# A gated convolution with its tokens on the partitions, two opening blocks that take turns, and a warm-up on a constant, in a two-layer decoder kernel

## Chip, cores and metric

One core of a Trainium2 chip runs the whole program. The metric is the device time of one execution in microseconds (us). The kernel before takes 259.68 us, the median of 3 runs (259.32 to 259.75).

## What is computed

Two layers on x (256 tokens, 1024 wide, fp32). Each layer normalizes its input, multiplies it by a wide input matrix, mixes, gates with a SiLU and multiplies by an output matrix; the result is added to x. Layer 0 mixes by a causal convolution of three taps, layer 1 by causal attention over 256 tokens (16 heads of 64, with normalized q and k and a distance bias).

```python
def short_conv_mixer(h, w_in, conv_w, w_out):
    b_gate, c_gate, xv, z = split(h @ w_in, 4)
    u = c_gate * xv
    conv = conv_w[0] * u[t-2] + conv_w[1] * u[t-1] + conv_w[2] * u[t]
    y = b_gate * conv * silu(z)
    return y @ w_out
```

## The kernel before

**Units and products.** All weights are cut into 80 units of 256 rows by 512 columns (`UNITS`, L23); four units make a block, which fills two PSUM banks, one for each half (t = 0, 1) of the tokens. Every fp32 operand is split into a high part that TensorE reads as it is and a low part: ScalarE (ACT) copies the high part (`whi`, L355), VectorE (DVE) subtracts it from the loaded weights (`wlo`, L362). Each unit then takes 12 products of 128x512: high by high, high by low and low by high, for two k tiles and two token halves (L419 to L421; L405 for the first unit). Layer 0 has 32 units of the input matrix in two halves (`hf`) of four blocks each, C, x, gate and B, then 8 of the output matrix; layer 1 likewise with 32 and 8.

**The convolution before.** A block's products leave tokens on the partitions. `scaled` (L475) and `times` (L480) make u = C times x; `conv` (L502) turns u with 8 transposes on TensorE (PE, L451), so that columns stand on the partitions and tokens along the row, and a shift by one or two tokens is an offset in the row: ScalarE multiplies by one tap (L512), VectorE adds the other two (L520). `gated` (L533) turns B times SiLU in another 8 transposes, multiplies (L539) and splits the result into high and low `ys` (L493, L497), the input of the output matrix.

**What sets the order.** The kernel records every operation with its engine, a cost, and what it reads and writes; `Plan.schedule` (L164) simulates the engines and fixes one order for each engine. On the chip each engine takes its instructions in exactly that order, and each waits on semaphores for what it needs. Buffers are rings: 4 of 1 MiB for loaded weights (`raw`, a pair of units each), 5 units each for `whi` and `wlo`. All transfers are issued by SyncE (SP), from one queue: first x, as eight transposed k tiles, with the first four units (L298), then pairs of units (L314), with x again, tokens on the partitions, as `h` between (L325).

**The start.** Eight products of zeros (`WARM`, L273) run before data is there. `zero` is written by VectorE (L270).

Of the kernel before, what the change touches and what calls it, by code (L numbers as in the profile page):

```python
# [8 lines left out]
F32 = mybir.dt.float32  # L9
# [24 lines left out]
NSM = 48  # L34
# [168 lines left out]
def hybrid_kernel(  # L203
    ctx: ExitStack,
    tc: tile.TileContext,
    first: bass.AP,
    xt: bass.AP,
# [45 lines left out]
    sm = one.tile([P, NSM], F32, name="sm")  # L253
# [3 lines left out]
    zero = one.tile([P, 512], mybir.dt.bfloat16, name="zero")  # L257
    one.tile([P, 16], F32, name="fill")
# [3 lines left out]
    kk2 = one.tile([P, 2, 4, 2, S], F32R, name="kk2")  # L262
    kT, klz = kk2[:, :, :, 0], kk2[:, :, :, 1]
    qT = one.tile([P, 2, 4, S], F32R, name="qT")
    vv = one.tile([P, 2, 4, 4, HD], F32R, name="vv")
    g0, g1, taps = sm[:, 0:8], sm[:, 8:16], sm[:, 16:40]
# [16 lines left out]
    firsts = [raw_t() for _ in range(4)]  # L283
    raws = {g: raw_t() for g in range(2, NU // 2)}

    def piece(k, a, b):
        o = 768 * (k % 2) + (NSM if k < 2 else 0)
        return firsts[k // 2]().rearrange("p a b -> p (a b)")[:, o + a : o + b]


    def load_first(k, parts="xw"):
        a, b = (0 if "x" in parts else S), (768 if "w" in parts else S)
        if k == 0 and a == 0:
            a = -NSM
        op(
            "SP",
            max(us(P * 4 * (b - a)), 480),
            lambda: sp.dma_start(piece(k, a, b), first[:, NSM + 768 * k + a : NSM + 768 * k + b]),  # L298
            w=[(firsts[k // 2], (k % 2, p)) for p in parts],
        )  # L300


    def w_in(u, ks):
        if u >= 4:
# [3 lines left out]
        return (firsts[u], (k, "w")), lambda: piece(2 * u + k, S, 768).rearrange("p (k f) -> p k f", f=512)  # L308

    def load_pair(g):  # L310
        op(
            "SP",
            us(P * 8192),
            lambda: sp.dma_start(raws[g](), w[2 * g - 4 : 2 * g - 2].rearrange("u p e -> p u e")),  # L314
            w=[(raws[g], 0), (raws[g], 1)],
        )

    load_first(0, "x")
    load_first(0, "w")
    for k in range(1, KT):  # L320
        load_first(k)
    op("DVE", 80, lambda: dve.tensor_copy(sm, piece(0, -NSM, 0)), r=[(firsts[0], (0, "x"))], w=["sm"])
    load_pair(2)
    for t in range(2):
        op("SP", us(P * 4096), lambda t=t: sp.dma_start(h[:, t], xt[:, t]), w=[("h", t, 0), ("h", t, 1)])  # L325
    for g in range(3, NU // 2):
        load_pair(g)
# [12 lines left out]
    for s in range(2):  # L340
        r2 = slice(HD - s * HD, P - s * HD)
        op("POOL", 950, lambda s=s, r2=r2: pool.memset(klz[r2, s].bitcast(F32), 0.0), w=[("klz0", s)])
# [4 lines left out]
    def split(u, parts=1):  # L347
        for i in range(parts):
# [18 lines left out]
    def split_x(k):  # L367
        key = [(firsts[k // 2], (k % 2, "x"))] + (["sm"] if k else [])
        g = lambda: g0[:, k : k + 1] if k else piece(0, -NSM, 1 - NSM)
        op(  # L370
            "ACT",
            500,
            lambda: act.activation(xs[:, k, 0], piece(k, 0, S), AF.Copy, scale=g()),  # L373
            r=key,
            w=[("xs", k, 0)],
        )
        op(
            "DVE",
            480,
            lambda: dve.scalar_tensor_tensor(  # L380
                xs[:, k, 1], piece(k, 0, S), g(), xs[:, k, 0].bitcast(F32), op0=ALU.mult, op1=ALU.subtract
            ),
            r=key + [("xs", k, 0)],
            w=[("xs", k, 1)],
        )
# [4 lines left out]
    def dense(kp, banks, x, xname):  # L390
        u = unit[0]
        unit[0] += 1
        if u < 4:
            for k in (2 * kp, 2 * kp + 1):
                split_x(k)
        split(u, 2 if u < 4 else 1)

        last = u == NU - 1


        def first_products(kk):
            wh, wl = his[u]()[:, kk], los[u]()[:, kk]
            for n, (i, m) in enumerate(((0, wh), (1, wh), (0, wl))):
                for t in range(2):
                    pe.matmul(  # L405
                        banks[t](), lhsT=x[:, kk, i, t * P : (t + 1) * P], rhs=m, start=(kk == 0 and n == 0), stop=False
                    )
# [15 lines left out]
        steps = [[(0, kk), (1, kk)] for kk in range(2)]  # L423
        if last:
            steps = [[(0, 0)], [(0, 1)], [(1, 0, 0), (1, 1, 0)], [(1, 0, 1), (1, 1, 1)]]
        for tk in steps:
# [3 lines left out]
                lambda tk=tk: first_products(tk[0][1]) if u == 0 else [product(*a) for a in tk],  # L430
# [60 lines left out]
    def split_y(y, j0, nj):  # L491
        js = range(j0, j0 + nj)
        op("ACT", 150 + 250 * nj, lambda: act.copy(ys[:, j0 : j0 + nj, 0], y()[:, 0:nj]), r=[y], w=[("ys", j, 0) for j in js])  # L493
        op(
            "DVE",
            180 + 280 * nj,
            lambda: dve.tensor_sub(ys[:, j0 : j0 + nj, 1], y()[:, 0:nj], ys[:, j0 : j0 + nj, 0].bitcast(F32)),  # L497
            r=[y] + [("ys", j, 0) for j in js],
# [3 lines left out]
    def conv(hf, i, us_):  # L502
        j0 = 4 * hf + 2 * i
        bank = transposed(lambda t: us_[t](), us_, [2 * i * P, (2 * i + 1) * P])
        c = bias_t()
        for jj in range(2):
            j = j0 + jj
            b = lambda jj=jj: bank()[:, jj * S : (jj + 1) * S]
            op(
                "ACT",  # L510
                440,
                lambda b=b, j=j, jj=jj: act.activation(c()[:, jj], b(), AF.Copy, scale=taps[:, 16 + j : 17 + j]),  # L512
                r=[bank, "sm"],
                w=[(c, jj)],
            )
            for d in (1, 2):
                op(
                    "DVE",
                    460,
                    lambda b=b, j=j, jj=jj, d=d: dve.scalar_tensor_tensor(  # L520
                        c()[:, jj, d:S],
                        b()[:, 0 : S - d],
                        taps[:, 8 * (2 - d) + j : 8 * (2 - d) + j + 1],
                        c()[:, jj, d:S],
                        op0=ALU.mult,
                        op1=ALU.add,
                    ),
                    r=[bank, "sm"],
                    w=[(c, jj)],
                )  # L530
        return c

    def gated(hf, i, c, qs):  # L533
        bank = transposed(lambda t: qs[t](), qs, [2 * i * P, (2 * i + 1) * P])
        y = y_t()
        op(
            "DVE",
            700,
            lambda: dve.tensor_mul(y(), c(), bank().rearrange("p (j s) -> p j s", s=S)),  # L539
            r=[(c, 0), (c, 1), bank],  # L540
            w=[y],
        )
        split_y(y, 4 * hf + 2 * i, 2)

    for hf in range(2):
        banks = block(xs, "xs")
# [3 lines left out]
        banks = block(xs, "xs")  # L550
        us_ = [times(banks[t], t, cs[t]) for t in range(2)]
        convs = [conv(hf, i, us_) for i in range(2)]
        banks = block(xs, "xs")
        sl = [scaled(banks[t], t, AF.Silu) for t in range(2)]
        banks = block(xs, "xs")
        qs = [times(banks[t], t, sl[t]) for t in range(2)]
        for i in range(2):
            gated(hf, i, convs[i], qs)
# [54 lines left out]
    def small_ones():  # L613
        dve.tensor_scalar(epsv, v1, EPS, None, op0=ALU.mult)
        dve.tensor_mul(gg, sm[:, 40:41], sm[:, 41:42])
# [11 lines left out]
    def queries_or_keys(name, bank, t):  # L627
# [30 lines left out]
        for s in range(2):  # L658
            r, r2 = slice(s * HD, s * HD + HD), slice(HD - s * HD, P - s * HD)
            if name == "k":  # L660
                hi = kT[r, s, :, ts]
                op("ACT", 680, lambda r=r, hi=hi: act.activation(hi, psv()[r], AF.Copy, scale=gg[r]), r=[tb, "gg"], w=[("k", t, s, 0)])
# [4 lines left out]
                        klz[r, s, :, ts], psv()[r], gg[r], hi.bitcast(F32), op0=ALU.mult, op1=ALU.subtract  # L667
                    ),
                    r=[tb, "gg", ("k", t, s, 0)],
                    w=[("kl", t, s)],  # L670
                )
                op("POOL", 640, lambda r2=r2, s=s, hi=hi: pool.tensor_copy(kT[r2, s, :, ts], hi.bitcast(F32)), r=[("k", t, s, 0)], w=[("k", t, s, 1)])
            else:
                hi = qT[r, s, :, ts]
                op("ACT", 600, lambda r=r, hi=hi: act.copy(hi, psv()[r]), r=[tb], w=[("q", t, s, 0)])
# [3 lines left out]
                    lambda r=r, r2=r2, s=s, hi=hi: dve.tensor_sub(qT[r2, s, :, ts], psv()[r], hi.bitcast(F32)),  # L679
                    r=[tb, ("q", t, s, 0)],  # L680
                    w=[("q", t, s, 1)],
# [34 lines left out]
    def pair(j, s2):  # L716
# [7 lines left out]
        def scores():  # L724
            for s in range(2):
                a, b, o = qT[:, s, jj, 0:P], qT[:, s, jj, P:S], sc[s]()
                o1 = o[:, 0:S].rearrange("p (i k) -> p i k", k=P)
                pe.matmul(o1, lhsT=a, rhs=kk2[:, s, jj, :, 0:P], start=True, stop=True)
                pe.matmul(o[:, S:512], lhsT=b, rhs=kT[:, s, jj], start=True, stop=False)  # L729
# [206 lines left out]
```

## Time and profile before

| what | us |
|---|---|
| runs: median (lowest to highest) | 259.68 (259.32 to 259.75) |
| the profiled execution, its own time | 259.06 |
| its span | 257.3 |
| PE busy | 251.8 |
| DVE busy | 188.7 |
| ACT busy | 163.3 |
| POOL busy | 49.7 |

The span runs from the first instruction of the program to the last; the execution's own time has 1.8 us more around it. Busy times add up each engine's instructions; they overlap, and an idle engine costs nothing if nobody waits for it. In a timeline row the first number is the start, the second the time, and what stands in brackets is how long the engine sat idle before, and what ended that. PE is TensorE's products, PEld its weight loads; SPq is the queue that issues transfers.

### The profile page before, as it was taken

To read this page: it belongs to the slowest core of one execution; us is meant where nothing else is said; L and a number is where in the kernel's file an instruction comes from. 1 tells how busy PE (TensorE), PEld (TensorE's weight loads), DVE (VectorE), ACT (ScalarE), POOL (GpSimd) and SP (SyncE) were. 2 spreads that over 40 slices of the span, in tenths; PEclk is the share of its full clock that TensorE was granted. 3 is DMA by queue.
4 is the path that set the end of the run, shared out by engine and by line. 5 is a ranking of instruction groups with operands and counts; after the bars stand their busy time and mean duration, and the time that the engine had idled before them with its cause. 6 is when DMAs were issued, how large, how long until landed. Compare 5 with 4: busy or idle time off the path is not lost.

```text
span 257.3 us, 3436 instructions
## 1 busy us (share of the span) xinstructions
PE 251.8 (98%) x1198; PEld 206.8 (80%) x1198; DVE 188.7 (73%) x335; ACT 163.3 (63%) x286; POOL 49.7 (19%) x76
## 2 busy tenths in 40 slices
PE   8999999999999999999999999999999999999994
PEld 3688888888888888888888888888888888888873
DVE  2874985575558458667767976984999899977973
ACT  4868655345445535474557668996887777988720
POOL 5001000000000000000636511242164901045230
PEclk9999999999999999999999999999999999999999
DMA  6999985554666444654655454053094504400004
GB/s 216 398 395 416 383 318 164 167 171 161 225 223 201 163 163 163 176 190 173 227 169 211 138 191 163 3 169 157 3 284 152 219 3 164 164 0 3 0 0 163
DMA packets 12657, 45.33 MB, mean 176 GB/s; under 512 B 864, under 2 KB 1248, under 8 KB 12640
## 3 DMA queue, kind: packets, MB, share of 16 engines
q1 hardware_dynamic: 12640, 45.12, 49.6%
q8 instruction: 9, 0.15, 0.2%
q14 instruction: 8, 0.07, 0.1%
HBM read 44.06 MB, written 1.05 MB: 175 GB/s over the span
## 4 chain that ended last, share of the span: by engine, by line
PE 87%; DVE 4%; ACT 3%; DMA 2%; issue 1%; POOLq 0%; SPq 0%; POOL 0%
PE mm L421 26%; PE mm L419 26%; PE mm L420 26%; DMA raw<-in_first_dram 2%; PE at L451 2%; PE at L799 2%; PE at L653 1%; DVE wlo L362 1%; DVE y L838 1%; ACT whi L355 1%; PE at L820 1%; ACT prob L761 1%; DVE pp L806 1%; PE at L730 1%; PE at L729 1%
## 5 line engine op out<-in xcount | busy, mean ns | idle before, releaser
L362 DVE TENSOR_TENSOR wlo<-raw,whi 128x1024 fp32r<-128x1024 f32 (+1 forms) x84 | 98.0, 1175 | 43.0 <-ACT whi L355 42.7
L355 ACT CAST whi<-raw 128x1024 fp32r<-128x1024 f32 (+1 forms) x84 | 84.5, 1012 | 69.7 <-PE mm L421 56.5
L419 PE MATMUL mm<-whi,xs 128*128 128x512 f32 x252 | 100.3, 398 | 0.2 <-ACT xs L373 0.2
L421 PE MATMUL mm<-whi,xs 128*128 128x512 f32 x252 | 98.5, 391 | 0.0
L420 PE MATMUL mm<-wlo,xs 128*128 128x512 f32 x252 | 98.3, 390 | 0.0
L421 PEld LDWEIGHTS mm<-whi,xs 128*128 128x128 f32 x252 | 47.3, 188 | 10.4 <-DVE xs L380 0.2
L419 PEld LDWEIGHTS mm<-whi,xs 128*128 128x128 f32 x252 | 47.4, 188 | 9.4 <-ACT xs L373 0.6
L420 PEld LDWEIGHTS mm<-wlo,xs 128*128 128x128 f32 x252 | 47.4, 188 | 9.0
L419 PE MATMUL mm<-whi,ys 128*128 128x512 f32 (+1 forms) x64 | 25.4, 397 | 0.0
L421 PE MATMUL mm<-whi,ys 128*128 128x512 f32 (+1 forms) x64 | 24.9, 389 | 0.3 <-POOL ys L844 0.3
L420 PE MATMUL mm<-wlo,ys 128*128 128x512 f32 (+1 forms) x64 | 24.7, 386 | 0.0
L459 POOL TENSOR_TENSOR stat<-stat,nhalf 128x2 f32<-128x2 f32 x2 | 1.4, 709 | 118.1 <-DVE stat L458 118.1
L838 DVE TENSOR_TENSOR y<-at,y 64x256 f32<-64x256 f32 x32 | 13.5, 421 | 4.6 <-ACT y L836 3.8
L721 POOL TENSOR_SCALAR bias<-dist 128x256 f32<-128x256 f32 x16 | 9.1, 569 | 30.5 <-DVE sums L751 28.5
L761 ACT ACTIVATE prob<-neg,sums 128x256 f32<-128x256 f32 (+1 forms) x32 | 14.3, 449 | 1.0 <-DVE sums L751 0.9
L421 PEld LDWEIGHTS mm<-whi,ys 128*128 128x128 f32 x64 | 12.0, 188 | 3.2 <-POOL ys L844 0.7
L420 PEld LDWEIGHTS mm<-wlo,ys 128*128 128x128 f32 x64 | 12.1, 188 | 2.1
L419 PEld LDWEIGHTS mm<-whi,ys 128*128 128x128 f32 x64 | 12.0, 188 | 2.0
L635 POOL TENSOR_TENSOR ss<-ss,nhalf 128x8 f32<-128x8 f32 x8 | 13.1, 1641 | 0.7
L844 POOL TENSOR_TENSOR ys<-y,ys 128x256 fp32r<-128x256 f32 x8 | 7.7, 962 | 18.1 <-ACT ys L840 18.1
L775 POOL TENSOR_TENSOR sg<-row,sums 128x128 f32<-128x128 f32 x16 | 7.1, 463 | 16.9 <-ACT row L711 10.6
L802 ACT CAST pp<-at 128x384 fp32r<-128x384 f32 x16 | 7.5, 480 | 2.0 <-PE at L799 1.9
(95 smaller groups left out, 260.8 us busy)
## 6 DMA issues: line engine op xcount, KB each, us to landing
raw<-in_w_dram SPq DMA_DIRECT2D x38, 1024.0 KB, 4.9
raw<-in_first_dram SPq DMA_DIRECT2D x7, 384.0 KB, 6.5
h<-in_x_dram SPq DMA_DIRECT2D x2, 512.0 KB, 8.2
out_dram<-row SPq DMA_DIRECT2D x3, 256.0 KB, 2.5
raw<-in_first_dram SPq DMA_DIRECT2D x1, 256.0 KB, 2.7
out_dram<-row SPq DMA_DIRECT2D x2, 128.0 KB, 2.2
raw<-in_first_dram SPq DMA_DIRECT2D x1, 152.0 KB, 2.6
```

The source lines that it names most:

```text
L355: lambda c=c, src=src: act.copy(his[u]()[:, c], src()),
L362: lambda c=c, src=src: dve.tensor_sub(los[u]()[:, c], src(), his[u]()[:, c].bitcast(F32)),
L419: pe.matmul(o, lhsT=a, rhs=wh, start=(k == first_k), stop=False)
L420: pe.matmul(o, lhsT=a, rhs=wl, start=False, stop=False)
L421: pe.matmul(o, lhsT=b, rhs=wh, start=False, stop=(k == KT - 1))
L635: pool.tensor_tensor(ss()[:, 8:16], ss()[:, 0:8], nhalf, op=ALU.pow)
L721: op("POOL", 450, lambda s=s, slope=slope: pool.tensor_scalar(b()[:, s], dist, slope, 1.0, op0=ALU.mult, op1=ALU.mult), r=["dist", "epsv"] ...
L761: lambda s=s, c=c, i=i, neg=neg: act.activation(p[s]()[:, c], neg()[:, c], AF.Exp, bias=sums()[:, i : i + 1], scale=-1.0, accum_out=sums() ...
L775: lambda t=t: pool.tensor_mul(sg()[:, t].rearrange("p (s d) -> p s d", d=HD), s2[t]()[:, jj * P : (jj + 1) * P].rearrange("p (s d) -> p s ...
L802: op("ACT", 480, lambda s=s, tb=tb: act.copy(pp()[:, s, 0], tb()[:, 0:384]), r=[tb], w=[(pp, (s, 0))])
L838: op("DVE", 430, lambda s=s, r=r, c=c: dve.tensor_add(y()[r, 1], av[s]()[r, c], y()[r, 1]), r=[av[s]], w=[(y, s)])
L844: lambda: pool.tensor_sub(ys[:, j, 1], y()[:, 0], ys[:, j, 0].bitcast(F32)),
```

## The change

**Start.** The first two blocks (units 0 to 3 and 4 to 7) take turns over the first four k tiles; then each runs its last two units alone. The first six units and x are loaded in pieces in the order of the table `FIRST`, where `x3` is a k tile of x and `(4, 1)` the second k tile of unit 4. The high part of k tile 0 is made by VectorE. The warm-up reads a constant of the program in place of `zero`.

**Convolution.** u stays as it comes, tokens on the partitions. A shift by d tokens is now a shift by d partitions, made by transfers inside SBUF: the "main" one moves 128 - d rows of 4 KB (both token halves), the "head" one d rows of 2 KB across the halves. Taps come from HBM, copied to every partition (1.5 MiB), and VectorE multiplies and adds on 128x1024. The gate follows, and one group of 8 transposes for each half remains, whose result goes straight to `ys`. The 8 transposes of u, L512 and L520 are gone.

```diff
+NF = 6
+FIRST = [
+    [[(0, 0)], ["p", "x0"], [(4, 0)]],
+    [["x1", (0, 1)], [(4, 1), "x2"]],
...
+    [["x6", (3, 0)], ["x7", (3, 1)]],
+]
-    dve.memset(zero, 0.0)
+    ones = lambda n: nc.const_aps.tensor(1.0, [P, n], mybir.dt.bfloat16)
-        pe.matmul(idle, lhsT=zero[:, 0:P], rhs=zero, start=True, stop=True)
+        pe.matmul(idle, lhsT=ones(P), rhs=ones(512), start=True, stop=True)
+    op("SP", us(P * 12288), lambda: sp.dma_start(early()[:, 0:3072].bitcast(F32), taps_b), w=[(early, "taps")])
...
+    def conv(hf, banks, cs):
...
+                    u_at(t), banks[t](), r0[:, t : t + 1], cs[t](), op0=ALU.mult, op1=ALU.mult
...
+        for d in (1, 2):
+            op(
+                "SP",
+                1400,
+                lambda d=d: sp.dma_start(u_before(d)[d:P], u_both()[0 : P - d]),
...
+            op(
+                "SP",
+                480,
+                lambda d=d: sp.dma_start(u_before(d)[0:d, 1], u_at(0)[P - d : P]),
...
+                lambda d=d: dve.tensor_mul(u_before(d), u_before(d), tb(2 - d)),
...
+        op("DVE", 1230, lambda: dve.tensor_mul(u_both(), u_both(), tb(2)), r=[(early, "taps")], w=[(early, ("u", t)) for t in range(2)])
...
+            lambda: dve.tensor_add(u_before(1), u_before(1), u_before(2)),
...
+            lambda: dve.tensor_add(u_before(1), u_before(1), u_both()),
...
+    def gated(hf, sl):
...
+                lambda t=t: dve.tensor_mul(sl[t](), sl[t](), u_before(1)[:, t]),
...
+    def output(hf, i, ys_):
+        bank = transposed(lambda t: ys_[t](), ys_, [2 * i * P, (2 * i + 1) * P])
...
+        op("ACT", 620, lambda: act.copy(ys[:, j0 : j0 + 2, 0], ps()), r=[bank], w=[("ys", j, 0) for j in js])
...
+    def first_blocks():
+        both = [[mm_t(), mm_t()] for _ in range(2)]
+        for k in range(4):
+            for i in range(2):
+                dense(k // 2, both[i], xs, "xs", 4 * i + k // 2, k % 2)
+        for i in range(2):
+            for kp in (2, 3):
+                dense(kp, both[i], xs, "xs", 4 * i + kp)
```

**Order on SP, before.** The whole queue of transfers; `raw` is the weight ring, `row` the output.

```order
L298 DMA raw<-in_first_dram 128x512
L298 DMA raw<-in_first_dram 128x304
L298 DMA raw<-in_first_dram 128x768 x7
L314 DMA raw<-in_w_dram 128x2x1024 x2
L325 DMA h<-in_x_dram 128x1024 x2
L314 DMA raw<-in_w_dram 128x2x1024 x36
L883 DMA out_dram<-row 128x512 x3
```

Every transfer here has 128 rows, one for each partition.

**Order on SP, changed,** from the last opening piece on. `kk` holds the taps and u, `qq` the shifted copies of u.

```order
L346 DMA raw<-in_w_dram 128x2x1024
L356 DMA h<-in_x_dram 128x1024 x2
L346 DMA raw<-in_w_dram 128x2x1024 x5
L354 DMA kk<-in_taps_dram 128x3072
L556 DMA qq<-kk 2x512
L549 DMA qq<-kk 126x1024
L556 DMA qq<-kk 1x16x32
L549 DMA qq<-kk 127x1024
L346 DMA raw<-in_w_dram 128x2x1024 x9
L549 DMA qq<-kk 127x1024
L556 DMA qq<-kk 1x16x32
L549 DMA qq<-kk 126x1024
```

The taps and the four shifts of the first half stand behind the pair of units 16 and 17, those of the second half behind the pair of units 34 and 35; 22 pairs follow.

**Order on DVE, before,** from the first u (L485) to the first gate (L539) of the first half.

```order
L485 SCALAR_TENSOR_TENSOR row<-mm,stat,row 128x512 x2
L362 TENSOR_TENSOR wlo<-raw,whi 128x1024 x3
L520 SCALAR_TENSOR_TENSOR bias<-at,sm,bias 128x255 x4
L362 TENSOR_TENSOR wlo<-raw,whi 128x1024
L520 SCALAR_TENSOR_TENSOR bias<-at,sm,bias 128x254 x3
L362 TENSOR_TENSOR wlo<-raw,whi 128x1024
L520 SCALAR_TENSOR_TENSOR bias<-at,sm,bias 128x254
L362 TENSOR_TENSOR wlo<-raw,whi 128x1024 x4
L485 SCALAR_TENSOR_TENSOR row<-mm,stat,row 128x512 x2
L362 TENSOR_TENSOR wlo<-raw,whi 128x1024
L539 TENSOR_TENSOR y<-bias,at 128x512
```

Nothing between u and the gate reads a transfer inside SBUF; L520 reads what PE has turned.

**Order on DVE, changed,** around the convolution of the first half: L539 makes u, L566 to L581 the taps, L591 the gate, L525 is B times that.

```order
L539 SCALAR_TENSOR_TENSOR kk<-mm,stat,row 128x512 x2
L390 TENSOR_TENSOR wlo<-raw,whi 128x1024 x4
L566 TENSOR_TENSOR qq<-qq,kk 128x1024
L390 TENSOR_TENSOR wlo<-raw,whi 128x1024
L566 TENSOR_TENSOR qq<-qq,kk 128x1024
L570 TENSOR_TENSOR kk<-kk 128x1024
L574 TENSOR_TENSOR qq<-qq 128x1024
L581 TENSOR_TENSOR qq<-qq,kk 128x1024
L591 TENSOR_TENSOR row<-row,qq 128x512 x2
L525 SCALAR_TENSOR_TENSOR row<-mm,stat,row 128x512 x2
L390 TENSOR_TENSOR wlo<-raw,whi 128x1024 x4
```

The first L566 reads the shift by two tokens, the second the shift by one. The splits (L390) ahead of L539 end with unit 12, the one between the two L566 is that of unit 17, and the first behind L525 that of unit 18. On PE the 8 transposes that read L525's result stand behind unit 16 in the first half and behind unit 32 in the second.

**Order on DVE, changed,** at the same place of the second half.

```order
L566 TENSOR_TENSOR qq<-qq,kk 128x1024
L390 TENSOR_TENSOR wlo<-raw,whi 128x1024
L566 TENSOR_TENSOR qq<-qq,kk 128x1024
L390 TENSOR_TENSOR wlo<-raw,whi 128x1024
L570 TENSOR_TENSOR kk<-kk 128x1024
L390 TENSOR_TENSOR wlo<-raw,whi 128x1024
L574 TENSOR_TENSOR qq<-qq 128x1024
L581 TENSOR_TENSOR qq<-qq,kk 128x1024
L591 TENSOR_TENSOR row<-row,qq 128x512 x2
L390 TENSOR_TENSOR wlo<-raw,whi 128x1024 x3
L525 SCALAR_TENSOR_TENSOR row<-mm,stat,row 128x512 x2
```

Here the first L566 reads the shift by one token, and the split behind it is that of unit 30; the three ahead of L525 are those of units 33 to 35.

## Rows read from the trace of the kernel before

**Rows 1.** The page: busy times, and the chain that ended last by engine.

```profile
PE 251.8 (98%) x1198; PEld 206.8 (80%) x1198; DVE 188.7 (73%) x335; ACT 163.3 (63%) x286; POOL 49.7 (19%) x76
...
PE 87%; DVE 4%; ACT 3%; DMA 2%; issue 1%; POOLq 0%; SPq 0%; POOL 0%
```

**Rows 2.** Timeline of PE, first 10 us: start, time, instruction, [idle before].

```profile
1.17 3.60 PE L273 MATMUL at<-zero 128*128 128x512 bf16 x8 [1.17 <-DVE nhalf L330]
4.57 1.96 PE L405 MATMUL mm<-whi,xs 128*128 128x512 f32 x4
...
8.78 0.50 PE L419 MATMUL mm<-whi,xs 128*128 128x512 f32 x1 [0.17 <-ACT xs L373]
...
9.83 0.39 PE L419 MATMUL mm<-whi,xs 128*128 128x512 f32 x1
```

**Rows 3.** Timeline of ACT: high parts of the weights (L355), and what they waited for.

```profile
14.88 2.00 ACT L355 CAST whi<-raw 128x1024 fp32r<-128x1024 f32 x2 [1.41 <-DMA raw<-in_w_dram]
17.44 2.00 ACT L355 CAST whi<-raw 128x1024 fp32r<-128x1024 f32 x2 [0.56 <-DMA raw<-in_w_dram]
...
22.50 1.05 ACT L355 CAST whi<-raw 128x1024 fp32r<-128x1024 f32 x1 [0.97 <-DMA raw<-in_w_dram]
...
28.42 1.06 ACT L355 CAST whi<-raw 128x1024 fp32r<-128x1024 f32 x1 [0.87 <-PE mm L421]
...
42.95 1.05 ACT L355 CAST whi<-raw 128x1024 fp32r<-128x1024 f32 x1 [0.51 <-PE mm L421]
45.67 1.05 ACT L355 CAST whi<-raw 128x1024 fp32r<-128x1024 f32 x1 [1.67 <-PE mm L421]
48.39 1.05 ACT L355 CAST whi<-raw 128x1024 fp32r<-128x1024 f32 x1 [1.67 <-PE mm L421]
```

**Rows 4.** Timeline of PE around the first transposes of u (L451).

```profile
30.95 1.04 PE L451 MATMUL at<-ident,row 128*128 128x128 f32 x8
31.74 0.47 PE L419 MATMUL mm<-whi,xs 128*128 128x512 f32 x1
32.05 0.39 PE L420 MATMUL mm<-wlo,xs 128*128 128x512 f32 x1
```

**Rows 5.** The DMA view: all packets, then issues with KB each and us to landing.

```profile
DMA packets 12657, 45.33 MB, mean 176 GB/s; under 512 B 864, under 2 KB 1248, under 8 KB 12640
...
raw<-in_w_dram SPq DMA_DIRECT2D x38, 1024.0 KB, 4.9
raw<-in_first_dram SPq DMA_DIRECT2D x7, 384.0 KB, 6.5
h<-in_x_dram SPq DMA_DIRECT2D x2, 512.0 KB, 8.2
out_dram<-row SPq DMA_DIRECT2D x3, 256.0 KB, 2.5
raw<-in_first_dram SPq DMA_DIRECT2D x1, 256.0 KB, 2.7
out_dram<-row SPq DMA_DIRECT2D x2, 128.0 KB, 2.2
raw<-in_first_dram SPq DMA_DIRECT2D x1, 152.0 KB, 2.6
```

**Rows 6.** Busy times by stretch: PE, PEld, DVE, ACT, POOL, granted clock, DMA share, GB/s.

```profile
20.00:26.00 6.00, 6.00 (x28) 4.95 (x28) 2.60 (x4) 5.03 (x9) 0.72 (x1) 1.00 1.03 420
...
38.00:60.00 22.00, 22.00 (x103) 18.28 (x102) 13.80 (x16) 10.25 (x12) 0.00 (x0) 1.00 0.55 183
```

**Rows 7.** Groups of DVE by form, first 110 us: count, busy, mean ns, idle before.

```profile
L362 DVE TENSOR_TENSOR wlo<-raw,whi 128x1024 fp32r<-128x1024 f32 x37 | 44.9, 1223 | 30.9 <-ACT whi L355 30.8
L485 DVE SCALAR_TENSOR_TENSOR row<-mm,stat,row 128x512 f32<-128x512 f32 x8 | 5.6, 744 | 0.0
...
L539 DVE TENSOR_TENSOR y<-bias,at 128x512 f32<-128x512 f32 x4 | 2.7, 684 | 1.7 <-PE at L451 1.7
```

**Rows 8.** Timeline of DVE: two splits in a row.

```profile
25.68 2.36 DVE L362 TENSOR_TENSOR wlo<-raw,whi 128x1024 fp32r<-128x1024 f32 x2 [0.87 <-ACT whi L355]
```

More of the change, by code (lines that the diff above doesn't have):

```diff
@@ L206, in hybrid_kernel @@
     first: bass.AP,
+    taps_b: bass.AP,
     xt: bass.AP,
@@ L256, in hybrid_kernel @@
     stat = one.tile([P, 24], F32, name="stat")
-    zero = one.tile([P, 512], mybir.dt.bfloat16, name="zero")
-    one.tile([P, 16], F32, name="fill")
+    one.tile([P, 272], F32, name="fill")
     h = one.tile([P, 2, DM], F32, name="h")
@@ L279, in us, with item, load_first @@
         return nbytes / 370
[L283 to L294, printed above, removed]
+    firsts = [raw_t() for _ in FIRST]
+    raws = {g: raw_t() for g in range(NF // 2, NU // 2)}
+    where = {}
+    base = 0
+    transfers = []
+    for f, groups in zip(firsts, FIRST):
+        o = 0
+        for group in groups:
+            o0 = o
+            for item in group:
+                where[item] = f, o, item_size(item)
+                o += item_size(item)
+            transfers.append((f, o0, o, base + o0, group))
+        base += o
+    def item(name):
+        f, o, n = where[name]
+        return f().rearrange("p a b -> p (a b)")[:, o : o + n]
+    def load_first(f, o0, o1, at, group):
         op(
             "SP",
-            max(us(P * 4 * (b - a)), 480),
-            lambda: sp.dma_start(piece(k, a, b), first[:, NSM + 768 * k + a : NSM + 768 * k + b]),
-            w=[(firsts[k // 2], (k % 2, p)) for p in parts],
+            max(us(P * 4 * (o1 - o0)), 480),
+            lambda: sp.dma_start(f().rearrange("p a b -> p (a b)")[:, o0:o1], first[:, at : at + o1 - o0]),
+            w=[(f, i) for i in group],
         )
     def w_in(u, ks):
-        if u >= 4:
+        if u >= NF:
             g = raws[u // 2]
@@ L388, in hybrid_kernel, with dense @@
     unit = [0]
-    def dense(kp, banks, x, xname):
-        u = unit[0]
-        unit[0] += 1
+    def dense(kp, banks, x, xname, u=None, only=None):
+        if u is None:
+            u = unit[0]
+            unit[0] += 1
         if u < 4:
-            for k in (2 * kp, 2 * kp + 1):
+            for k in (2 * kp, 2 * kp + 1) if only is None else (2 * kp + only,):
                 split_x(k)
-        split(u, 2 if u < 4 else 1)
+        split(u, 2 if u < NF else 1, only)
         last = u == NU - 1
[L401 to L407, printed above, removed]
         def product(t, kk, half=None):
@@ L421, in product @@
             pe.matmul(o, lhsT=b, rhs=wh, start=False, stop=(k == KT - 1))
-        steps = [[(0, kk), (1, kk)] for kk in range(2)]
+        if only is not None and 2 * kp + only == 0:
+            wh, wl = lambda: his[u]()[:, 0], lambda: los[u]()[:, 0]
+            for n, (i, m, parts) in enumerate(((0, wh, his), (1, wh, his), (0, wl, los))):
+                op(
+                    "PE",
+                    454,
+                    lambda n=n, i=i, m=m: [
+                        pe.matmul(banks[t](), lhsT=x[:, 0, i, t * P : (t + 1) * P], rhs=m(), start=(n == 0), stop=False)
+                        for t in range(2)
+                    ],
+                    r=[(parts[u], 0), (xname, 0, i)],
+                    w=banks,
+                    rank=1,
+                )
+            return
+        steps = [[(0, kk), (1, kk)] for kk in ((0, 1) if only is None else (only,))]
         if last:
@@ new lines, in gated @@
+    def gated(hf, sl):
+        for t in range(2):
+            op(
+                "DVE",
+                700,
+                lambda t=t: dve.tensor_mul(sl[t](), sl[t](), u_before(1)[:, t]),
+                r=[(shifted, (1, p)) for p in ("zero", "main", "head")],
+                w=[sl[t]],
+            )
+    def output(hf, i, ys_):
+        bank = transposed(lambda t: ys_[t](), ys_, [2 * i * P, (2 * i + 1) * P])
+        j0 = 4 * hf + 2 * i
+        ps = lambda: bank().rearrange("p (j s) -> p j s", s=S)
+        js = (j0, j0 + 1)
+        op("ACT", 620, lambda: act.copy(ys[:, j0 : j0 + 2, 0], ps()), r=[bank], w=[("ys", j, 0) for j in js])
```

221 lines of the change are left out of this document (118 added, 103 removed).

## The prediction

> **What bounds the kernel now.** I read the page first: PE is busy for 251.8 of 257.3 us and carries 87% of the chain that ended last [rows 1]. A change can therefore gain only by taking work off PE or by filling the places where PE waits, and can lose by making PE wait. The next question is where it waits. In the timeline of PE the eight warm-up products start 0.43 us apart (3.40 us from 1.17 to 4.57), and the first 15 products (12 of L405 and three more), from 4.57 to 9.83, take 5.26 us [rows 2]. From then on the pace is that of the units: ScalarE starts a new split every 2.72 us, each time released by PE, which has freed a buffer [rows 3]. So a unit of 12 products takes 2.72 us, one product 0.227 us, and the opening 15 products would take 3.4 us at that pace: 1.9 us are lost at the start. After the start loads and splits are ahead of PE (ScalarE waits for PE, not for data, from 28.42 on [rows 3]), and PE is full in both stretches shown, the second of which is convolution [rows 6]. Last the DMA view and the stretches: from 20 to 26 us the transfers run at full rate, 420 GB/s on all 16 DMA engines (share 1.03), from 38 to 60 us at about half [rows 6].
>
> **The start.** The second block gives PE six more products for each k tile that arrives, in the very gap where it now waits (0.17 us before 8.78, and the slow pace around it [rows 2]). Bounds: nothing, if the lower pace of the first products simply lasts longer; 1.9 us, if all is recovered. I take 1.0: the first product still needs the first piece and its high part, and the first products still come at the slow pace. Dropping `zero` lets the warm-up begin up to 0.4 us earlier; this is inside the same bound. The copies, pieces and the extra DVE operation for k tile 0 lie beside loads that are late anyway.
>
> **PE work of the convolution.** Each of the two halves loses one group of 8 transposes. A group takes 0.79 us from its start to the next product (30.95 to 31.74), and that product then takes 0.31 us instead of 0.23 to the next [rows 4]: 0.87 us, twice, is 1.75 us. PE is full there, so all of it counts. The ScalarE copies and VectorE multiply-adds that go are off the path, and both engines have idle time there [rows 6]; they are costed at nothing.
>
> **The shifts.** This is the added wait. The DVE operation on a shifted copy waits for a transfer issued by SP, and behind it on DVE stand the splits of later units and, at last, the operation that PE's remaining transposes need. What does a shift by one token cost? It moves 127 rows of 4 KB. No row of the trace moves 127 rows, so I bound it. The trace has 54 transfers (38+7+2+3+1+2+1) and 864 packets under 512 B [rows 5]: 864 is 54 times 16, one closing packet from each of the 16 DMA engines for every transfer. All have 128 rows, so each engine gets an equal share of 8. At 420 GB/s an engine moves 26 GB/s [rows 6], a row of 4096 B in 0.156 us. If 127 rows are spread as 128 are, the shift moves in 8 x 0.156 = 1.3 us. If shares must be equal in whole rows, 127, a prime number, has only one engine to go to: 127 x 0.156 = 19.8 us. I take 19.8, because equal shares are what all 54 transfers show; the 126 rows of the other shift then go to 14 engines, 9 each, 1.4 us. The Trainium skill says the same from another side: by "DMA: Bandwidth & Descriptors", section "Why a DMA increments its semaphore by 16 and not by 1", a transfer uses the largest number of engines, up to 16, that divides the outermost dimension, and it names 127 partitions as a case for one engine. The trace agrees for 128 rows and cannot show 127; by that rule the sum below is 287, with the nearest rows taken as they stand it is 257.
>
> **First half.** Bytes ahead of the pair of units 8 and 9 are as before, so it lands near 22.5 again [rows 3]; a pair is 1.05 MB, 2.5 us at 420 GB/s. Units 10 to 17 follow until 32.5, the taps (1.57 MB) until 36.2, then the shift by two (1.4 us), then the 127 rows: 37.6 + 19.8 = 57.4. u is earlier than that: unit 7 ends at 28.4 - 1.0 = 27.4 [rows 3], then come the high part (1.05 [rows 3]) and low part (1.2 [rows 7]) of unit 12, and u itself (2 x 0.74 [rows 7]), 31.2 in all, so the queue and not u sets the shift. VectorE goes on from 57.4 with four operations on 128x1024 (1.18 each, as two splits in a row take 2.36 [rows 8]), two of 0.69 and two of 0.74 us [rows 7], together 7.6: 65.0. PE reaches the transposes after unit 16, at 27.4 + 9 x 2.72 = 51.9. It waits 13.1 us.
>
> **Second half.** After the transposes (0.87) PE does units 17 to 23 (19.0), 84.9; with a slower restart (below, 1.3) 86.2. u takes 1.5, 87.7. The shift by one is first in its group now and the queue is half empty [rows 6]: 128 KB land 2.2 us after issue, of which 0.3 is moving [rows 5], so 1.9 + 19.8 later, 109.4. DVE stands at this shift; the split of unit 30 is behind it. From there to the operand of the transposes are five operations and six splits of 1.18 and four short ones, 15.9 us: 125.3. PE would have come to them, after units 24 to 32, at 86.2 + 24.5 = 110.7. It waits 14.6 us.
>
> **Restart.** After a wait of 13 us PE may come back at the pace of the start, 0.43 us a product. The start bounds this: from 1.17 until at most 6.5 us it ran so [rows 2], half of which is lost: between 0 and 2.6 us at each of two waits; I take 1.3. The Trainium skill, "TensorE: Matmul & The Clock Gate", section "Part 1: The HAM clock gate", says that idleness puts the clock back to half; no row here shows it after the start. Without that the sum would be 2.6 less.
>
> **Sum.** -1.0 - 1.75 + 13.1 + 14.6 + 2.6 = +27.6. The profiled execution took 259.06 us, so 286.6; the median of the runs is 0.6 above it, so I forecast **287 us**. Layer 1 is reordered slightly by the planner; I cost that at nothing, because PE's products there are the same.
>
> **The range of this case.** Low: both restarts free (-2.6), the start wholly recovered (-0.9), and the 127 rows begun alongside the taps and not after them (-5.1): 278. High: rows that take a third longer inside SBUF than from HBM (13 in two shifts) and the full restart (2.6): 302.
>
> **Rivals.**
> 1. *The 127 rows go to all 16 engines, unevenly.* Then a shift lands near 36.2 + 2 x 1.3 = 38.8. DVE wants it after the low part of unit 17, whose buffer is free after unit 12 (27.4 + 5 x 2.72 = 41.0, plus 1.05 and 1.2): 43.3. Nothing waits, the sum is -2.75, and the time 256.9: faster. For it: every row of the trace uses all 16. Against: every row is a multiple of 16.
> 2. *Spread, but late all the same.* VectorE needs 7.6 us from 43.3, 50.9, and PE is there at 51.9: a margin of 1.0 us. If queueing behind weights and taps delays the shift beyond 44.4, each us more is a us on PE; from 47 on the gain is gone. A shift at 48 would give about 260: the same, or slower. Against: it must land 9 us later than its bytes need.
> **How the numbers follow.** One engine: 0.83. Rival 1: 0.11. Rival 2: 0.04. The rest, 0.02, is something slower still. A measurement of this kernel tells about 0.2% from no change, 0.5 us. Faster is rival 1 and a little: 0.11; the same, out of rival 2: 0.02; slower: 0.87. The range 278 to 302 holds nearly all of the first case, 0.79 in all, so it needs no stretch to 257.
>
> **What would show it.** The SP-issued L549 with 127 rows should land some 20 us after it starts moving, and DVE should sit idle before L566 until about 57 and 109. PE should stand before L491 near 52 and 111. The DMA share should fall far below 0.5 in these stretches, and PE's next products should come 0.43 us apart. The L491 groups should be two in place of four, and unit 7 should end near 27.4. If L549 lands within 3 us, the forecast is wrong by its main term, and 257 is the time; if PE waits but far less than 27 us in sum, the place of the shift in the queue was wrong.

## The result: 13.6% slower

The changed kernel takes **294.79 us** (median of 4 runs, 294.58 to 295.09) against 259.50 of the kernel before, measured beside it (4 runs): a ratio of 1.136, 95% interval 1.134 to 1.138. The forecast was 287 (278 to 302), slower with a chance of 0.87. The profiled execution took 294.58, with a span of 292.8.

The page of the changed kernel: busy times, the granted clock in 40 slices, the DMA share, the chain that ended last (by engine, then by line), and three groups (busy, mean ns | idle before, releaser).

```profile
PE 255.7 (87%) x1182; PEld 208.5 (71%) x1182; DVE 194.9 (67%) x330; ACT 160.2 (55%) x279; POOL 55.8 (19%) x81
...
PEclk9999999755899997589999999999999999999999
...
DMA  6999918900746251048564464540704372530003
...
PE 52%; DMA 24%; DVE 13%; issue 4%; ACT 3%; SPq 2%; POOLq 0%; POOL 0%; DVEq 0%; ACTq 0%
DMA qq<-kk 18%; PE mm L445 15%; PE mm L443 15%; PE mm L444 15%; DVE wlo L390 4%; DMA raw<-in_w_dram 3%; DMA raw<-in_first_dram 2%; DVE y L920 2%; PE at L491 2%; PE at L881 1%; ACT whi L383 1%; PE at L735 1%; DVE kk L539 1%; DVE qq L566 1%; DVE qq L581 1%
...
L444 PE MATMUL mm<-wlo,xs 128*128 128x512 f32 x252 | 100.2, 398 | 12.6 <-DVE wlo L390 12.6
...
L566 DVE TENSOR_TENSOR qq<-qq,kk 128x1024 f32<-128x1024 f32 x4 | 4.9, 1222 | 39.5 <-DMA qq<-kk 39.5
...
L491 PE MATMUL at<-ident,row 128*128 128x128 f32 x16 | 3.5, 359 | 18.4 <-DVE row L525 18.3
```

PE carried 87% of the chain [rows 1]; now it carries 52, and the shifts (`qq<-kk`) alone 18. VectorE waits 39.5 us for two of them, and PE 12.6 + 18.3 us for VectorE. The holes in the DMA line and the two dips of PEclk mark the places. PE's busy time grew although 16 transposes went: part of its products ran at the lower clock (0.5 in the rows below, 1.2 GHz; 1.00 is 2.4 GHz).

The chain of waits in order of time, around both shifts (start, us, what):

```profile
34.61 27.74 DMA qq<-kk
62.37 1.23 DVE qq L566
...
94.30 24.94 DMA qq<-kk
```

The second of these is the head of the second half, 2 KB: issued right behind the 127 rows (93.62), its last share landed at 119.24, 0.2 us after theirs (119.05).

Four stretches (PE, PEld, DVE, ACT, POOL busy, granted clock, DMA share, GB/s):

```profile
39.00:45.00 6.00, 6.00 (x29) 4.95 (x27) 3.71 (x4) 3.27 (x4) 0.00 (x0) 1.00 0.07 26
...
53.00:62.00 9.00, 0.09 (x1) 0.00 (x0) 0.00 (x0) 0.00 (x0) 0.00 (x0) 0.62 0.66 232
62.00:69.00 7.00, 0.00 (x0) 0.00 (x0) 6.56 (x7) 3.64 (x4) 1.03 (x2) 0.50 0.07 28
...
109.00:119.00 10.00, 0.19 (x1) 0.00 (x0) 0.00 (x0) 1.04 (x1) 0.00 (x0) 0.71 0.22 79
```

From 39 to 45 us only the shift moves: 26 GB/s and a share of 0.07, one engine of sixteen (1/16 is 0.06). [Rows 6] had 420 GB/s at 1.03.

The timeline of SP there: start, us, the transfers that it issues.

```profile
34.61 1.43 SPq L549 DMA_DIRECT2D qq<-kk  x1
36.14 11.20 SPq L346 DMA_DIRECT2D raw<-in_w_dram  x2
...
93.62 0.63 SPq L549 DMA_DIRECT2D qq<-kk  x1
94.30 9.11 SPq L556 DMA_DIRECT2D qq<-kk  x1
```

The timeline of DVE: the operations on the shifted copies, with the idle time before each in brackets.

```profile
62.37 1.23 DVE L566 TENSOR_TENSOR qq<-qq,kk 128x1024 f32<-128x1024 f32 x1 [17.81 <-DMA qq<-kk]
...
119.36 1.22 DVE L566 TENSOR_TENSOR qq<-qq,kk 128x1024 f32<-128x1024 f32 x1 [21.65 <-DMA qq<-kk]
```

The timeline of ACT in the first half, the first split of weights after the shift was issued and its wait:

```profile
64.90 1.99 ACT L383 CAST whi<-raw 128x1024 fp32r<-128x1024 f32 x2 [21.59 <-DMA raw<-in_w_dram]
```

The timeline of PE around the first wait:

```profile
52.71 0.39 PE L445 MATMUL mm<-whi,xs 128*128 128x512 f32 x1
69.27 2.32 PE L491 MATMUL at<-ident,row 128*128 128x128 f32 x8 [16.17 <-DVE row L525]
71.24 0.78 PE L443 MATMUL mm<-whi,xs 128*128 128x512 f32 x1
71.81 0.63 PE L444 MATMUL mm<-wlo,xs 128*128 128x512 f32 x1
72.24 0.63 PE L445 MATMUL mm<-whi,xs 128*128 128x512 f32 x1
```

PE comes back at 0.43 us a product. Two things were not in the forecast. SP stands for 9 us over its next issues. And ScalarE waits 21.6 us for a pair of weights: the pair issued right behind the shift. Whether this second wait has a price of its own is a question for the experiments.

### The profile page after: what moved, and what is told of

Its sections match the earlier page's. It is cut to its first block, busy times and chain, and to the rows that moved or that the text cites. A ratio compares the mean times of both kernels' runs of the same rounds, so it can differ in the third digit from the quotient of the medians.

```text
span 292.8 us, 3422 instructions
## 1 busy us (share of the span) xinstructions
PE 255.7 (87%) x1182; PEld 208.5 (71%) x1182; DVE 194.9 (67%) x330; ACT 160.2 (55%) x279; POOL 55.8 (19%) x81
## 3 DMA queue, kind: packets, MB, share of 16 engines
HBM read 45.63 MB, written 1.05 MB: 159 GB/s over the span
## 4 chain that ended last, share of the span: by engine, by line
PE 52%; DMA 24%; DVE 13%; issue 4%; ACT 3%; SPq 2%; POOLq 0%; POOL 0%; DVEq 0%; ACTq 0%
DMA qq<-kk 18%; PE mm L445 15%; PE mm L443 15%; PE mm L444 15%; DVE wlo L390 4%; DMA raw<-in_w_dram 3%; DMA raw<-in_first_dram 2%; DVE y L920 2%; PE at L491 2%; PE at L881 1%; ACT whi L383 1%; PE at L735 1%; DVE kk L539 1%; DVE qq L566 1%; DVE qq L581 1%
## 5 line engine op out<-in xcount | busy, mean ns | idle before, releaser
L390 DVE TENSOR_TENSOR wlo<-raw,whi 128x1024 fp32r<-128x1024 f32 (+1 forms) x86 | 98.7, 1163 | 35.7 <-ACT whi L383 35.4
L444 PE MATMUL mm<-wlo,xs 128*128 128x512 f32 x252 | 100.2, 398 | 12.6 <-DVE wlo L390 12.6
L443 PE MATMUL mm<-whi,xs 128*128 128x512 f32 x252 | 102.0, 405 | 0.1
L445 PE MATMUL mm<-whi,xs 128*128 128x512 f32 x252 | 100.1, 397 | 0.0
L444 PEld LDWEIGHTS mm<-wlo,xs 128*128 128x128 f32 x252 | 48.6, 193 | 22.5 <-DVE wlo L390 13.0
L445 PEld LDWEIGHTS mm<-whi,xs 128*128 128x128 f32 x252 | 48.3, 192 | 10.7 <-DVE xs L412 0.2
L443 PEld LDWEIGHTS mm<-whi,xs 128*128 128x128 f32 x252 | 48.5, 192 | 9.9 <-ACT xs L403 0.6
L566 DVE TENSOR_TENSOR qq<-qq,kk 128x1024 f32<-128x1024 f32 x4 | 4.9, 1222 | 39.5 <-DMA qq<-kk 39.5
L491 PE MATMUL at<-ident,row 128*128 128x128 f32 x16 | 3.5, 359 | 18.4 <-DVE row L525 18.3
L491 PEld LDWEIGHTS at<-ident,row 128*128 128x128 f32 x16 | 2.4, 179 | 19.7 <-POOL qq L534 16.6
L640 POOL MEMSET kk<- 64x1024 f32 x2 | 1.9, 951 | 60.4 <-DMA raw<-in_w_dram 60.3
L717 POOL TENSOR_TENSOR ss<-ss,nhalf 128x8 f32<-128x8 f32 x8 | 13.1, 1641 | 0.7
```

The source lines that it names most:

```text
L390: lambda c=c, src=src: dve.tensor_sub(los[u]()[:, c], src(), his[u]()[:, c].bitcast(F32)),
L443: pe.matmul(o, lhsT=a, rhs=wh, start=(k == first_k), stop=False)
L444: pe.matmul(o, lhsT=a, rhs=wl, start=False, stop=False)
L445: pe.matmul(o, lhsT=b, rhs=wh, start=False, stop=(k == KT - 1))
L491: pe.transpose(bank()[:, (2 * i + t) * P : (2 * i + t + 1) * P], src(t)[:, c : c + P], ident)
L566: lambda d=d: dve.tensor_mul(u_before(d), u_before(d), tb(2 - d)),
```

## Experiments

The theory: a transfer from SP's queue is spread in equal shares of whole rows, so 127 rows lie on one engine, and VectorE's wait for them stops PE. Ten experiments were run, on nine kernels; each time stands against runs of the kernel before on the same chip (259.03 to 259.26).

### The rows: split shifts

```diff
-    lambda d=d: sp.dma_start(u_before(d)[d:P], u_both()[0 : P - d]),
+    lambda d=d: [
+        sp.dma_start(u_before(d)[d + a : d + b], u_both()[a:b]) for a, b in ((0, 112), (112, P - d))
+    ],
```

> Edit: each long shift (126 and 127 rows) is moved as two transfers, rows 0 to 111 and the 14 or 15 rows behind them; nothing else changes. Theory (a transfer is spread in equal shares of whole rows, so 127 rows have one engine): 112 rows are 7 on each of 16 engines, 15 rows 1 on each of 15; both parts of a shift land within 3 us of their start, L566 no longer waits (39.5 us of idle time in the changed kernel go below 2), PE's pauses before L491 (16.3) and before unit 30's second products (12.75) go, and 294.8 becomes about 258 (257 to 260). Rival (a move from SBUF to SBUF is slow whatever its rows, or the two DVE operations and the queue are what costs): the transfers still take some 20 us, and the time stays above 285.

Measured: 256.48 us (6 runs), ratio 0.9904 (0.9881 to 0.9927). The page of this kernel, busy times and the chain by engine:

```profile
PE 249.3 (98%) x1182; PEld 205.5 (81%) x1182; DVE 195.1 (77%) x330; ACT 160.2 (63%) x279; POOL 55.8 (22%) x81
...
PE 90%; DVE 5%; ACT 2%; issue 1%; POOLq 0%; POOL 0%; ACTq 0%
```

Its waits (us in total, times, longest):

```profile
DVE qq L568 <- DMA qq<-kk: 2.0, 2, 1.7
```

The same bytes and operations in four transfers more take 38 us less: 39.5 us of VectorE's wait became 2.0. Moving inside SBUF is not slow in itself. The order of instructions on PE and VectorE is that of the changed kernel. This version also beats both kernels. A second measurement of it, below, gives 257.45. (The two pauses that the expectation gives as 16.3 and 12.75 are 16.17 and 12.59 in the trace.)

### The rows: divisors

The shift by one goes as 124 + 3 rows in the first half and 122 + 5 in the second:

```diff
+        sp.dma_start(u_before(d)[d + a : d + b], u_both()[a:b]) for a, b in (((0, 124 - 2 * hf), (124 - 2 * hf, 127)) if d == 1 else ((0, 126),))
```

> Edit: the shift by one is moved as 124+3 rows in the first half and as 122+5 rows in the second. Theory (the number of engines is the largest up to 16 that divides the rows): 124 rows have 4 engines with 31 rows each, 31 x 0.156 = 4.8 us; 122 rows have 2 engines with 61 each, 9.5 us; 3 and 5 rows have as many engines, one row each. The completions of the 124 rows come from 4 engines at about 5 us after the start, those of the 122 from 2 at about 10 us. The first half then does not wait on PE (0 to 1 us), the second little (0 to 2 us): 258 to 261. Rival (one engine only because the number is odd, any even number gets 16 or 14): both land within 3 us and the time equals that of the split shifts. Rival (rows are dealt out 16 at a time and the rest goes to one engine): 124 and 122 rows land within 3 us as well, and so would 127 have, which the changed kernel denies.

Measured: 269.69 us (4 runs), ratio 1.0405 (1.038 to 1.043). The trace records each update of a transfer's semaphore, which counts to 16. For a transfer with fewer than 16 separate updates, one more comes within 2 us of the issue; it is read here as standing for the idle engines. The others come one by one. Those others, from five kernels:

```
kernel        rows  queue  issued  updates  first and last (us)
changed        127  SP      34.61        1  62.35
changed        126  SP      33.11       14  37.83  39.30 
split          112  SP      32.46       16  36.66  39.88
split           15  SP      35.97       15  39.34  41.97
124+3          124  SP      35.73        4  46.24  48.65
122+5          122  SP      77.38        2  91.90  92.84
ScalarE queue  127  ACT     34.02        1  67.91
POOL           127  POOL    33.04       16  37.76  42.16
```

On SP's queue the number of engines is the largest up to 16 that divides the rows: 16, 15, 14, 4, 2, 1. Both rivals fall. This is the rule of the Trainium skill's "DMA: Bandwidth & Descriptors", section "Why a DMA increments its semaphore by 16 and not by 1", and the trace agrees in every row of SP.

The expected time (258 to 261) was missed by 9 us. The 31 rows of an engine were to take 4.8 us and took about 7 to 9, the 61 rows 11 to 12: while they move, the pairs of weights issued behind them move on the same engines. VectorE waits 16.3 us in place of 39.5, and PE still pauses three times for some 2.8 us. A long share is not only long, it is slowed by what follows it. The three pauses add up to some 8 us, and the granted clock fell to 0.5 twice, for 3.4 us each (from 95.84 and from 109.50).

### The queue: ScalarE's and POOL's

```diff
-                "SP",
+                "ACT" if d == 1 else "SP",
...
-                lambda d=d: sp.dma_start(u_before(d)[d:P], u_both()[0 : P - d]),
+                lambda d=d: (act if d == 1 else sp).dma_start(u_before(d)[d:P], u_both()[0 : P - d]),
```

> Edit: the changed kernel with the 127-row transfers alone issued by ScalarE's queue instead of SP's. Theory (equal shares of whole rows, whatever queue): still one engine for 127 rows, L566 still waits some 20 us, PE still pauses before L491, 280 to 295; but the weight pairs are no longer behind it in one queue, so SP is not held for 9 us, and the sixteenth part of a pair lands within 6 us of the others. Rival (the one engine is a matter of SP's queue): 257 to 260.

Measured: 304.95 us (2 runs), ratio 1.1768 (1.1747 to 1.1788), 10 us slower still, and above the expected range. It is still one engine (the table), but SP is no longer held: the pair issued at 34.65 landed in 15 parts by 43.35 and in the sixteenth at 47.69, 4 us later and not 15 (the pair issued at 39.12: 9 us). In exchange the engine now serves both queues, and the shift lands 33.9 us after its issue, where it took 27.7. The waits of this kernel:

```profile
DVE qq L566 <- DMA qq<-kk: 49.4, 2, 25.1
...
PE mm L444 <- DVE wlo L390: 32.5, 2, 17.2
```

So the one engine doesn't belong to SP's queue alone; on ScalarE's the same rows go to one engine too. For POOL the edit is the same with `"POOL"` and `pool`:

> Edit: the changed kernel with the 127-row transfers alone issued by POOL. Theory (equal shares of whole rows, whatever queue): one engine, 280 to 295. Rival (POOL deals rows out to the engines itself, unevenly where it must): the 127 rows land within 4 us, PE does not pause, 257 to 260.

Measured: 257.31 us (2 runs), ratio 0.9929 (0.9910 to 0.9949). The theory as written falls for this queue: the rival was right in its main point and its time, though the rows landed 9.1 us after their issue and not within 4; VectorE waits 5.7 us for the shifts, and PE does not pause. This kernel and the one before it have the same order of instructions on PE, VectorE and ScalarE (the first transposes stand six products later than in the changed kernel), so the queue is what separates 304.95 from 257.31. The DMA view of this kernel, packets, MB and share of POOL's queue:

```profile
q0 software_dynamic: 288, 1.04, 1.4%
```

Two transfers, 144 packets each. The packets of the 127 rows of the first half lie between 35.2 and 41.5 us, and their times add up to 30.6 us: many engines moved them side by side. On ScalarE's queue they lie between 38.3 and 67.6 us and add up to 22.0, one behind the other. That POOL used all 16 engines is read from its 16 separate updates. The same section of the Trainium skill names this exception for some direct copies issued by POOL on this chip; the trace agrees.

### The wait that nobody names: what stands behind on the queue

First the shift's readers were taken away:

```diff
+    dead = one.tile([P, 2, 2, 512], F32, name="dead")
...
+                lambda d=d: sp.dma_start((spare(0) if d == 1 else u_before(d))[d:P], u_both()[0 : P - d]),
...
+                lambda d=d: dve.tensor_mul(u_before(d), u_both() if d == 1 else u_before(d), tb(2 - d)),
...
+        op("DVE", 1230, lambda: dve.tensor_mul(spare(1), u_both(), tb(2)), r=[(early, "taps")] + [(early, ("u", t)) for t in range(2)], w=[("dead", 1)])
```

> Edit: the changed kernel, its 127-row transfer as before, but into a tile that nothing reads, and u is not overwritten (the product with the last tap goes to a second spare tile), so no engine waits for it; the multiply of the shift by one reads u itself, so this kernel leaves the shift by one out of the convolution. Theory A (the price is the wait of VectorE for the shifted copy, nothing else): PE does not pause, 256.5 to 259. Theory B (the transfer also holds up the weights: in the changed kernel the pair issued behind it, at 36.14, landed in 15 parts by 50.0 and in the 16th at 64.80, and ScalarE stood 21.6 us for it): PE pauses before the products of the next unit until about 66 instead of 69, some 13 us after unit 17, and 0 to 12 us in the second half: 270 to 287.

Measured: 279.94 us (4 runs), ratio 1.0806 (1.0789 to 1.0822). The order moved the first transfer behind four pairs, to 50.19, so the place of the pauses differs from the one expected; the size is that of theory B. But the kernel isn't clean: in the second half VectorE waited 7.3 us to overwrite u, which the first transfer was still reading, and 3.6 us for the other shift, which stood behind the transfer. So a pair of kernels was run that differ in one row:

```diff
+        op(
+            "SP",
+            1400,
+            lambda: sp.dma_start(dead[0:127], early()[0:127, 0:1024].bitcast(F32)),
+            r=[("ready", hf), (early, "taps")],
+            w=["dead"],
+        )
```

> Edit: the kernel with split shifts, and in each half one more transfer of 127 rows of the taps (which nothing overwrites) into a tile that nothing reads; no engine waits for it at any time. Its partner differs by one row (128). Theory (a transfer on one engine also holds up the weight pairs issued behind it on SP's queue, whose sixteenth part lies on that engine): the pair behind lands in 15 parts and some 15 us later in the 16th, ScalarE stands for it, PE pauses for 5 to 15 us in each half, 265 to 285. Rival (what nobody waits for costs nothing but 0.5 MB of transfer): 256 to 258.5.

> Edit: as its partner, with 128 rows in place of 127 in the transfer that nobody waits for. Both theories: 16 engines, 8 rows each, landing within 4 us of its start, no pause of PE, 256 to 258.5; the difference to the partner is the price of one row less.

Measured: 279.60 us (4 runs, ratio 1.0786, 1.0761 to 1.0812) with 127 rows, 258.96 (10 runs, ratio 0.9992, 0.9965 to 1.0019) with 128. One row less costs **20.6 us**, though neither PE nor VectorE nor ScalarE waits for the transfer itself. The order of instructions on these engines and on SP is the same in both. With 128 rows it is slightly above the bound given; the last products come later in both kernels of the pair (in that with 128 rows, 226.0 us from the 96th product to the last after 222.7 in the split kernel), so this isn't the row. The timeline of ACT in the kernel with 127 rows:

```profile
84.44 1.99 ACT L384 CAST whi<-raw 128x1024 fp32r<-128x1024 f32 x2 [12.77 <-DMA raw<-in_w_dram]
...
124.06 1.04 ACT L384 CAST whi<-raw 128x1024 fp32r<-128x1024 f32 x1 [12.61 <-DMA raw<-in_w_dram]
```

The pair issued behind the first transfer, at 59.63, landed in 15 parts by 68.4 and in the sixteenth at 84.34. With 128 rows its counterpart, issued at 59.36, was whole at 64.03. A transfer on one engine delays that engine's share of everything behind it, and a pair of weights is split by ScalarE only when its last share is there.

Two more waits of this kernel (us in total, times, longest):

```profile
POOL kk L650 <- DMA dead<-kk: 66.1, 1, 66.1
...
DVE qq L576 <- DMA qq<-kk: 6.4, 1, 6.4
```

POOL does wait for the second transfer, contrary to the expectation, to overwrite the tile that it reads; what POOL writes there is for layer 1, and the trace shows nobody waiting for it. VectorE waits 6.4 us (2.1 with 128 rows) for the split shifts of the second half: they stand behind the first transfer as the weights do. So the 20.6 us are the price of everything behind the two transfers, the weights and these shifts, and not of the weights alone.

### The start

```diff
-NF = 6
+NF = 4
...
-        for k in range(4):
-            for i in range(2):
-                dense(k // 2, both[i], xs, "xs", 4 * i + k // 2, k % 2)
...
+        for u in range(1, 8):
+            dense(u % 4, both[u // 4], xs, "xs", u)
```

This diff, with the former order of pieces, undoes the turns in the kernel with split shifts; another kernel has the new start with the former convolution; and the split shifts were measured once more.

> Edit: the changed kernel's start (two blocks by turns, its order of pieces, the constant warm-up) with the former convolution, transposes and taps in the small table. By the prediction's term the start is worth -1.0 us (0 to -1.9): 258.5. By the changed kernel's trace the 96th product starts at 28.45, after 28.22 before, so the start gives nothing: 259.3 to 260.0, not to be told from 259.5.

> Edit: as the kernel with split shifts, and the start's order undone (first one block, then the other, pieces in the former order; the high part of k tile 0 and the constant warm-up stay as changed). By the prediction's term for the start this is 1.0 us slower than the split shifts with the turns; by the changed kernel's trace it is the same or up to 0.3 us faster. Against the kernel before it shows what the 16 transposes are worth: -1.75 us by the prediction, so 257.8; by a rival (what PE no longer transposes it waits for elsewhere) 259.5.

> The kernel with split shifts once more, for its start. In its first profile the fourth piece of the start landed at 6.41 us on its last engine and the 96th product began at 26.94; in the changed kernel, with the same start, at 7.87 and 28.23. Theory (how late the slowest DMA engine delivers the first pieces differs from execution to execution, and the start gains about 1.2 us when it is early and nothing when it is late): the runs fall near 256.0 and near 257.2, and this profile shows one of the two. Rival (the early start belongs to this kernel): all near 256.0 and the fourth piece by 6.5.

Measured: the start alone 259.52 us (12 runs, ratio 1.0027, 1.0007 to 1.0048), no gain. Split shifts without the turns 257.64 (5 runs, ratio 0.9939, 0.9923 to 0.9955): 1.4 us less than before, near the -1.75 of the prediction for the transposes, and not the rival's nothing. Split shifts again 257.45 (6 runs, ratio 0.9926, 0.9912 to 0.9941). (The 28.45 and 28.22 in the first expectation are starts of the 97th product, one later than the 96th used here.) The 12 runs of the kernel with split shifts lie between 255.93 and 257.79, spread out and not in two heaps. Both forms of the last expectation miss in that, but the profiles agree with its cause. The fourth transfer of the start carries k tile 1 (`x1` and the second k tile of unit 0). In the ten profiles of kernels with this start it lands, on its last engine, between 6.41 and 8.33 us, and the 96th product begins 20.3 to 20.5 us later in each:

```
                      fourth transfer landed   96th product began
split                          6.41                   26.94
POOL                           7.50                   27.83
changed                        7.87                   28.23
start alone                    7.98                   28.29
split, again                   8.33                   28.62
```

The kernel before had 27.99. What the turns are worth thus goes with the slowest of 16 engines in the first 8 us: about 1 us at best, often nothing. No run changed this landing alone, and an engine that is late with this piece is late with the next ones too (8.14 after 6.41, 9.26 after 8.33), so which piece decides stays open. Why it is early in one execution and late in another wasn't tried.

## Why the prediction was right, and where its sizes were off

The main term was right, and its rival 1 (127 rows unevenly on 16 engines) was wrong for SP's queue, though it is what POOL does. Rival 2 asked whether a shift spread over 16 engines comes in time: in the split kernel VectorE waits 2.0 us and PE does not pause, so its margin held. Of the prediction's signs, L549 lands 27.7 us after its issue, some 23 after its rows begin to move, VectorE stands before L566, PE before L491, the DMA share falls to 0.07, products come back 0.43 us apart, and two groups of L491 remain. Unit 7 did not end early.

Measured against the sum (27.6 predicted; 294.58 - 259.06 = 35.5 measured):

| step | predicted | measured |
|---|---|---|
| the start | -1.0 (0 to -1.9) | +0.2: the 96th product at 28.23 after 27.99 |
| 16 transposes less | -1.75 | -1.9: the 385 products from the 96th on, 89.96 us in the split kernel, 91.90 before |
| first wait | +13.1 | +16.2 [16.17 before L491] |
| second wait | +14.6 | +14.7: 12.6 before a product of unit 30, 2.1 before L491 |
| restart, twice | +2.6 (0 to 5.2) | +5.8: 3.3 and 2.5 |

These come to 35.0; 0.5 us are not assigned. The 8 us between forecast and result lie almost wholly in three terms that were mis-sized:

- **The restart (+3.2).** "I take 1.3" at each wait, the middle of its bounds. The granted clock stood at 0.5 from 55.21 to 75.69 and from 113.24 to 126.89, so PE ran at the lower level for some 6 us after the first wait, from 69.27, transposes included, and for 5 after the second. The upper bound, 2.6, was the better value, and the transposes, which also ran at this level (1.97 us for 0.87), took the first restart above it. PE had done nothing from 53.1 on when the clock fell. The rule of the Trainium skill's "TensorE: Matmul & The Clock Gate", section "Part 1: The HAM clock gate", that idleness puts it back to half, is what these rows show.
- **The first wait (+3.1).** The rows began to move at about 39, not 37.6, and took some 23 us, not 19.8, so they landed at 62.35, 4.9 us late. The pace of 0.156 us a row held while the shift was alone (26 GB/s from 39 to 45 us); from 45.5 on the next pair of weights shared the engine. Against this, VectorE's operations up to the transposes took 6.9 us and not 7.6, and PE was there at 53.1 and not at 51.9.
- **The start (+1.2).** "I take 1.0". The turns were to fill the gap before the next piece; in this execution that piece came as late as before.

The second wait had the right size at another place. The prediction let PE run to the transposes after unit 32; in fact the low part of unit 30, which it had named as standing behind L566 on VectorE, stopped PE first. That its size came out is partly luck: the shift landed 25.6 us after its issue and not 21.7 (its rows began at about 96.7, behind a pair of weights, and took some 22 us), while the 2.5 us of the second restart fell between the two parts of this wait and shortened the second.

One step was missing, and the total hid it. The prediction asked who waits for the shift and what is queued behind the waiting instruction on VectorE; it didn't ask what is queued behind the *transfer* on SP. There stood the weights of unit 18. Their last share landed at 64.80, and with ScalarE's and VectorE's splits PE could not have had them before about 67 (64.9 + 1.05 + 1.2), where the shift released it at 69.3. The two waits ran side by side, so the second cost nothing here; the pair with 127 and 128 rows shows that what is held up behind such transfers costs 20.6 us with nobody waiting for their rows. The kernel without the reader, unclean as it is, won back less than half (279.94).

The expected gain of the change was real: with the shifts split, the kernel takes 1.8 to 2.6 us less than the one before in two measurements; the transposes are 1.9 by the traces, and the start gives up to 1.

## What to carry to other kernels

- Before moving part of a tile, look at the number of rows: on SP's queue it needs a large divisor up to 16 (127 rows went to one engine on ScalarE's queue too). 127 rows as 112 + 15, and 126 as 112 + 14, turned 294.8 into 256.5 us.
- A transfer costs twice: at its reader, and at everything behind it that needs a share of the same engines. Count what is issued next on the queue, even if nothing waits for the transfer itself.
- A gain at the start of a kernel needs more than one profile: here it went with the landing of the early pieces, the fourth at 6.4 to 8.3 us.

## What was not expected of the hardware

- SP was held some 9 us over the issues behind a one-engine transfer (9.11 us for one of 2 KB), and the pair behind it, issued at 36.14, moved nothing until 45.5, although 15 engines were idle. Behind the transfers of 127 rows that nobody reads the longest holds were 3.8 to 11.2 us. With the shift on ScalarE's queue this didn't happen. Why SP is held wasn't tried.
- The granted clock fell after much shorter pauses than those of the changed kernel: in the kernel with 122 + 5 rows it went to 0.5 after a pause of 2.8 us before PE's product at 95.75, and stayed there for 3.4 us; after one of the same length before 55.79 it didn't fall. In the kernel with 128 rows it fell at 243.13, after pauses of 0.9, 0.4 and 0.5 us from 239.9 on.
